# A hybrid decoder layer on one core: output weights split once into device memory, opening output groups started early, SP loads reordered

## The chip, the core and the metric

The kernel runs on one core of a Trainium2 chip. The core has five engines with instruction streams of their own: TensorE (PE, matmuls from SBUF into PSUM), VectorE (DVE), ScalarE (ACT), GpSimd (POOL) and SyncE (SP, which here only issues DMAs). ACT and POOL issue DMAs too. The metric is device time in microseconds of one execution, lower is better. Before the change it is 1189.5 us, the median of three runs.

## The reference

One decoder layer for 1024 prompt tokens and 8 x 8 sample tokens (1088 in all), model width 1024, float32. One input projection feeds two mixers, retention (8 heads of 64, in chunks of 128 tokens) and sliding-window attention (8 query heads, 2 key heads, window 128, with sinks). Their outputs, side by side, go through one output projection with a residual, and then comes an MLP of width 4096 with squared ReLU:

```
o_r = rms_norm(retention(q_r, k_r, v_r)) * silu(g_r)
o_s = sliding_window_attention(q_s, k_s, v_s, sinks)
h = x + concatenate([o_r, o_s], axis=-1) @ w_out
hf = rms_norm(h, norm_ffn_gain)
y = h + square(relu(hf @ w_up)) @ w_down
```

The retention state and the last window of keys and values are outputs too.

## The kernel before

Everything is kept with features on partitions and tokens along the free side. A float32 product is made of three matmul passes on operands of type float32r: each operand is split into a high part (an ACT cast) and a low part (DVE or POOL subtracts the high part), and `mm3` (lines 174 to 177) multiplies high by high, low by high and high by low.

The stages follow each other in the program, but a planner in the tile library orders each engine's instructions at build time by a simulated clock and the program's order as priority. Tiles with one tag share a fixed number of places (`bufs`). A tile in a reused place waits until the readers of the earlier tile are done. Pools on one side of SBUF are stacked, and a pool opened after another was closed takes the same space. `tc.issue_after(x)` puts the instructions traced in its block behind `x` on `x`'s engine.

The order of the program:

1. Projections for the attention part, then eight window-attention blocks, `swa_block` (line 378). Each uses two score tiles `s` (ring of 3 places of 4 KB per partition) and two transposed tiles `pt` (ring of 2). Then the sample tokens' attention with one more `s` tile, `s8` (line 464).
2. Projections of retention queries, keys and gates, which are stored in device memory (lines 509 to 528). They also serve PE as work while the attention chain waits for the other engines. Then `attn.close()`.
3. Retention. Its pools `ret` and `retv` take the space of the attention pools. `ret_load` (line 540) brings a block's queries, keys and gates on the SP queue. Nine value blocks (`value_block`, line 590) and the sample tokens' steps (`retention_decode`) are put in a written order on PE with `queued`. `retention_block(t)` (line 698) does eight blocks in sequence, because each uses the state of the one before it: cast and subtraction of queries and keys (lines 705 to 710), scores, decay, values, state, then a norm (`head_norm`, line 611). `mix_block` (line 766) transposes the result, multiplies by the gate and splits it into the mix operands `mix[s, "rh"]` and `mix[s, "rl"]`.
4. The output projection, in two halves of tokens, `s` = 0 and 1, each in 8 groups `m` of 128 output features. A group has two PSUM tiles (`h` = 0, 1) and, for each, 12 matmuls with the attention mix (`"a"`) and 12 with the retention mix (`"r"`). The first half needs the mix of blocks 0 to 4 only, and its groups are put between blocks 5, 6 and 7 with `out_early`; the second half follows when retention is done. The attention mix comes back from device memory with `mix_load`.
5. The MLP, `up` for 16 pairs and then the down projection, which make up most of the span.

The weights of the output projection reach it so: `wo_pair` (line 819) loads 512 KB of two groups' raw rows on SP into a `raw` tile and splits each with `wsplit` (ACT cast, DVE subtraction, ring `wa` of 4). As both token halves need all weights, each raw weight is loaded and split twice, 32 splits of 128 x 512 in all. `wo_pair`'s pool `mw` is opened after `proj.close()`, in the space of the projection weights. The first raw loads of the up projection (line 1073 on, `r0` and `s56`) use the same `raw` ring of `mw`.

Of the kernel before, what the change touches and what calls it, by code (L numbers as in the profile page):

```python
# [11 lines left out]
F32 = mybir.dt.float32  # L12
F32R = mybir.dt.float32r
# [7 lines left out]
P = 128  # L21
# [15 lines left out]
def hymba_layer(ctx: ExitStack, tc: tile.TileContext, a: dict, o: dict):  # L37
# [90 lines left out]
    g_d = scratch.tile([P, 4, T], F32, name="g_d")  # L128
    ms_hi_d = scratch.tile([P, 4, T], F32, name="ms_hi_d")
    ms_lo_d = scratch.tile([P, 4, T], F32, name="ms_lo_d")  # L130
    y_d = scratch.tile([P, 4, 4, 2, Q], F32, name="y_d")
    u_d = [scratch.tile([P, 2, 2, 7, Q], F32, name=f"u_d{g}") for g in range(8)]

# [302 lines left out]
            )  # L436


    pr = psB.tile([P, 512], F32, tag="t2", name="prq8")
    for t4 in range(4):  # L440
        col_sums(pr[:, t4 : t4 + 1], q8s[:, t4, :], ones[:, 0:1])
# [19 lines left out]
        nc.sync.dma_start(d_, a[s_])  # L461
    nc.sync.dma_start(o["kc"][:, :, 0:120], kc[:, :, 8:128])
    nc.sync.dma_start(o["vc"][0:120], vc[8:128])
    s8 = sp.tile([P, 4, 256], F32, tag="s", name="s8", bufs=3)[:, :, :192]
    for tt in range(2):
        ps = psB.tile([P, 512], F32, tag="t1", name="sc8")
        for t4 in (2 * tt, 2 * tt + 1):
# [230 lines left out]
    def retention_block(t):  # L698
        nonlocal state
        nm = f"r{t}"  # L700
        vt = vts[t]
        qt, kt, gt = ret_load(t, ((rv, 2), (mxr, 1) if t in (3, 6) else (rv, 2)))

        pts = []
        nc.scalar.copy(kh, kt)
        nc.gpsimd.tensor_tensor(kl, kt, kh.bitcast(F32), ALU.subtract)
        for hh in range(2):
            q_ = slice(hh * 64, hh * 64 + 64)
            nc.scalar.copy(qbh[q_, :, hh, :], qt[q_])
            nc.vector.tensor_tensor(qbl[q_, :, hh, :], qt[q_], qbh[q_, :, hh, :].bitcast(F32), ALU.subtract)  # L710
        for i in range(2):
            ps = psB.tile([P, 512], F32, tag="t1", name="rs" + nm)
            for p_ in (2 * i, 2 * i + 1):
                cc = (p_ % 2) * 256
                mm3(ps[:, cc : cc + 256], kh[:, p_, :], kl[:, p_, :], qbh[:, p_, :, :], qbl[:, p_, :, :], True, True)
            pt = rp.tile([P, 4, 128], F32, tag="rpt", name="rpt" + nm, bufs=3)
            nc.vector.tensor_tensor(
                pt, ps.rearrange("p (h l) -> p h l", h=4), intra[:, 4 * i : 4 * i + 4, :], ALU.mult
            )
            pts += [pt[:, h, :] for h in range(4)]  # L720
        kd, _ = scaled_keys(kt, kdec, nm)

        po = psB.tile([P, 512], F32, tag="t3", bufs=1, name="ro" + nm)
        for h in range(8):
            for q_ in (slice(0, 64), slice(64, 128)):
                nc.tensor.matmul(
                    po[q_, h * 64 : h * 64 + 64], pts[h][:, q_], vt[:, h * 64 : h * 64 + 64],
                    start=h == 0, stop=h == 7 and t == 0,
                )
        if t:  # L730
            qd = rv.tile([P, 4, 128], F32, tag="qd", name="qd" + nm, bufs=1)
            nc.gpsimd.tensor_tensor(qd, qt, qdec, ALU.mult)
            for p_ in range(4):
                nc.tensor.matmul(
                    po[:, p_ * 128 : p_ * 128 + 128], qd[:, p_, :],
                    state[:, p_, :, :].rearrange("p h e -> p (h e)"), start=False, stop=p_ == 3,
                )
        pu = psB.tile([P, 512], F32, tag="t2", name="pu" + nm)
        for h in range(8):
            q_ = slice((h % 2) * 64, (h % 2) * 64 + 64)  # L740
            nc.tensor.matmul(
                pu[q_, (h // 2) * 64 : (h // 2) * 64 + 64], kd[:, h * 64 : h * 64 + 64], vt[:, h * 64 : h * 64 + 64],
                start=True, stop=True,
            )
        puv = pu[:, :256].rearrange("p (q e) -> p q e", q=4)
        new = states[t % 2]
        for hh in range(2):
            q_ = slice(hh * 64, hh * 64 + 64)
            if t == 0:
                nc.vector.tensor_copy(new[q_, :, hh, :], puv[q_])  # L750
            else:
                for p_ in range(4):
                    nc.vector.scalar_tensor_tensor(
                        new[q_, p_, hh, :], state[q_, p_, hh, :], sdec[q_, p_ : p_ + 1], puv[q_, p_, :],
                        ALU.mult, ALU.add,
                    )
        state = new
        if t == NB - 1:
            for hh in range(2):
                nc.sync.dma_start(o["st"][hh * 64 : hh * 64 + 64], state[hh * 64 : hh * 64 + 64, :, hh, :])  # L760

        mt = rv.tile([P, 512], F32, tag="mt", name="mt" + nm)
        head_norm(po, mt, slice(0, 128), nm)
        return mt, gt
# [42 lines left out]
        return raw  # L807


    mix, acc, fs, last_out = {}, {}, {}, [None]  # L810

    def mix_load(s, pl):
        for x, d_ in zip("hl", (ms_hi_d, ms_lo_d)):
# [4 lines left out]

    def wo_pair(s, m, half):

        raw = mw.tile([P, 1024], F32, tag="raw", name=f"wo{half}{s}_{m}_raw", bufs=3)
        c0 = 512 * (half == "a")
        nc.sync.dma_start(
            raw.rearrange("p (m n) -> p m n", m=2), a["w_out"][m : m + 2, :, c0 : c0 + 512].rearrange("m p n -> p m n")
        )
        for i in range(2):
            yield wsplit(raw[:, i * 512 : i * 512 + 512], "wa", f"wo{half}{s}_{m + i}", nc.vector)

    def out_half(s, half, ps, h, w, first, last):
        for k in range(4):  # L830
# [4 lines left out]
    def residual(s, m, pss):  # L835
        y = om.tile([P, 2, Q], F32, tag="y", name=f"y{s}_{m}", bufs=2)
        nc.gpsimd.dma_start(y.rearrange("p h n -> p (h n)"), a["xY"][:, s, m, :])
        for h in range(2):
            nc.vector.tensor_tensor(y[:, h, :], pss[h], y[:, h, :], ALU.add)
        kk, k2 = m % 4, m // 4  # L840
        nc.gpsimd.dma_start(y_d[:, 2 * k2 : 2 * k2 + 2, kk, s, :], y)
        if m > 5 and s == 0:
            f = mx0.tile([P, 2, Q], F32, tag=f"f{m}", name=f"f{s}_{m}")
        else:
            f = om.tile([P, 2, Q], F32, tag=f"f{min(m, 4)}", name=f"f{s}_{m}", bufs=1 + m // 4)
        fs[s, m] = f
        nc.scalar.activation(f, y, AF.Copy, scale=g_ffn[:, m : m + 1])

        def squares():
            if m == 0:  # L850
                acc[s] = mw.tile([P, 2, Q], F32, tag="acc", name=f"acc{s}")
                nc.scalar.activation(acc[s], y, AF.Square)
            else:
                sq = om.tile([P, 2, Q], F32, tag="sq", name=f"sq{s}_{m}")
                nc.scalar.activation(sq, y, AF.Square)
                nc.vector.tensor_tensor(acc[s], acc[s], sq, ALU.add)

        return squares
# [55 lines left out]
            nc.scalar.copy(rsf[:, s, h, :], pb[:, :Q])  # L914


    def queued(ins, f, *args):
        with tc.issue_after(ins):
            return f(*args)
# [24 lines left out]
    qbh, qbl, kh, kl = split_space([ring.tile([P, 1024], F32R, tag="raw", name=f"qk{i}", bufs=3) for i in range(3)])  # L944
    for i, x in enumerate("hl"):
        mix[0, "r" + x] = slot(6 + i, F32R, "mixr" + x)[:, : 8 * Q].rearrange("p (k h n) -> p k h n", k=4, h=2)
    held, mxr, mxrx = {}, None, ExitStack()
    for t in range(5):
        if t == 0:
            for _ in range(2):  # L950
# [8 lines left out]
        if t == 3:  # L959
            sl8c = slot(8, F32R, "qkb")  # L960
            qbh, qbl, kh, kl = split_space([sl8c[:, i : i + 1024] for i in (0, 1024, 2048)])
        if t:
            mix_block(t - 1, *held[t - 1])
        held[t] = retention_block(t)
        if 0 < t < 4:
            ins = queued(ins, value_block, t + 4)
    proj.close()
    mw = ctx.enter_context(pool("mw", side="right"))
    rsf = mw.tile([P, 2, 2, Q], F32, tag="rsf", name="rsf")
    ox = ExitStack()  # L970
    om = ox.enter_context(pool("o", side="right"))
    for x in "hl":
# [1 line left out]
    mxA = ox.enter_context(pool("mxA", side="right"))  # L974
    mx0x = ExitStack()
    mx0 = mx0x.enter_context(pool("mx0", side="right"))
    early = lambda: psA.tile([P, 512], F32, tag="mm", name="pso")[:, :Q]

    def out_early(m):

        if m and m % 2 == 0:
            gens["a"], gens["r"] = (wo_pair(0, m, x) for x in "ar")
            ahead.extend(next(gens[x]) for x in "ar")
        wa_, wr_ = ahead
        ahead.clear()
        if m % 2 == 0:
            ahead.extend(next(gens[x]) for x in "ar")
        pss = [early() for h in range(2)]
        for h in range(2):
            out_half(0, "a", pss[h], h, wa_, True, False)  # L990
            out_half(0, "r", pss[h], h, wr_, False, True)
        residual(0, m, pss)()

    gens = {x: wo_pair(0, 0, x) for x in "ar"}
    ahead = [next(gens[x]) for x in "ar"]
    mix_block(4, *held[4])
    for t in (5, 6, 7):
        mt = retention_block(t)
        for m in (2 * t - 10, 2 * t - 9):
            out_early(m)  # L1000
        if t == 6:
            with tc.issue_after(last_load[0].ins):
                mix_load(1, mxA)
        mix_block(t, *mt)
# [394 lines left out]
```

## Time and profile before

| what | value |
|---|---|
| median of three runs | 1189.5 us (1188.86 to 1191.59) |
| profiled execution: its time | 1188.43 us |
| profiled execution: its span, first to last instruction | 1186.7 us |
| granted TensorE clock | 1.00 |
| attention blocks end | about 263 us |
| retention and first output half | about 290 to 450 us |
| MLP begins | about 496 us |

The profile shows one execution. Busy times of the engines overlap, and a busy PE is not PE at its peak, since the end of a matmul is modelled and matmuls overlap in its pipeline. So stretches are read by the number of matmuls in them and by the waits of PE, not by PE's share alone. In a row of instructions, "x" counts them, `out<-in` names the tiles, and the bracket gives the idle time before and what ended it.

### The profile page before, as it was taken

What the parts mean: (1) busy time and instruction counts of PE and PEld (TensorE: products, weight loads), DVE (VectorE), ACT (ScalarE), POOL (GpSimd) and SP (SyncE); (2) the same over time, 40 slices, a digit from 0 to 9 for tenths busy, and PEclk for the clock granted to TensorE, in tenths of its full rate; (3) what the DMA queues carried; (4) which work ended last, traced back from release to release, by engine and by line L of the source; (5) the groups of instructions that cost most, each with busy time, mean ns of one, the idle gap of its engine ahead of it and who ended that gap; (6) DMA issues with size and microseconds to landing.
All of it is one profiled execution on the core that took longest, in us unless ns stands there. A gap on an engine that the chain in (4) does not pass through costs nothing.

```text
span 1186.7 us, 23488 instructions
## 1 busy us (share of the span) xinstructions
PE 1169.6 (99%) x9405; PEld 1123.5 (95%) x9405; DVE 839.1 (71%) x1546; ACT 513.8 (43%) x1055; POOL 494.2 (42%) x393
## 2 busy tenths in 40 slices
PE   8999999999999999999999999999999999999998
PEld 7999988989778899999999999999989999999998
DVE  7556868632257769887766667666788787888676
ACT  8343544553334347644444444444642333333231
POOL 0125333332255542467666666566383142053000
PEclk9999999999999999999999999999999999999999
DMA  7221235333525555343444434444685456443225
GB/s 247 73 62 68 93 102 166 104 115 98 180 74 168 181 183 156 113 156 133 141 151 148 144 130 141 151 148 157 236 290 157 148 169 203 143 155 104 76 59 187
DMA packets 102277, 169.44 MB, mean 143 GB/s; under 512 B 12000, under 2 KB 68256, under 8 KB 101912
## 3 DMA queue, kind: packets, MB, share of 16 engines
q1 hardware_dynamic: 88807, 123.80, 31.5%
q10 hardware_dynamic: 10800, 35.23, 9.3%
q0 software_dynamic: 2560, 8.91, 2.3%
q8 instruction: 74, 1.21, 0.4%
q14 instruction: 36, 0.29, 0.1%
HBM read 114.30 MB, written 53.61 MB: 142 GB/s over the span
## 4 chain that ended last, share of the span: by engine, by line
PE 81%; DVE 6%; DMA 5%; issue 3%; ACT 2%; POOL 2%; SPq 0%; ACTq 0%; DVEq 0%; POOLq 0%
PE psd L176 9%; PE psd L177 9%; PE psd L175 9%; PE psx L175 5%; PE psx L177 5%; PE psx L176 5%; PE psz L175 2%; PE psz L177 2%; PE psz L176 2%; PE pst L175 2%; PE pst L176 2%; PE pst L177 2%; PE psf L175 2%; PE psf L177 2%; PE psf L176 2%
## 5 line engine op out<-in xcount | busy, mean ns | idle before, releaser
L175 PE MATMUL psd<-uh,wd_w 128*128 128x272 f32 x896 | 258.4, 288 | 3.2 <-DVE a L1267 2.4
L176 PE MATMUL psd<-uh,wd_w 128*128 128x272 f32 x896 | 259.3, 289 | 0.0
L177 PE MATMUL psd<-ul,wd_w 128*128 128x272 f32 x896 | 257.9, 288 | 0.7 <-DVE ul L792 0.7
L175 PEld LDWEIGHTS psd<-uh,wd_w 128*128 128x128 f32 x896 | 169.1, 189 | 4.3 <-DVE a L1267 3.4
L177 PEld LDWEIGHTS psd<-ul,wd_w 128*128 128x128 f32 x896 | 168.7, 188 | 0.9 <-DVE ul L792 0.9
L176 PEld LDWEIGHTS psd<-uh,wd_w 128*128 128x128 f32 x896 | 168.4, 188 | 0.0
L1267 DVE TENSOR_TENSOR a<-a,psd 128x272 f32<-128x272 f32 x248 | 101.9, 432 | 48.9 <-PE psd L177 48.8
L792 DVE TENSOR_TENSOR wu_w<-wu_s,wu_w 128x512 fp32r<-128x512 f32 x64 | 61.9, 971 | 49.8 <-ACT wu_w L791 49.2
L791 ACT CAST wd_w<-wd_s 128x512 fp32r<-128x512 f32 x64 | 37.5, 621 | 119.0 <-PE psd L177 107.2
L792 DVE TENSOR_TENSOR ul<-ur,uh 128x1088 fp32r<-128x1088 f32 x56 | 84.0, 1527 | 4.1 <-ACT uh L791 4.1
L1120 DVE SCALAR_TENSOR_TENSOR m<-m,rsf 128x272 f32<-128x272 f32 x96 | 72.9, 760 | 3.2 <-ACT rsf L914 0.5
L175 PE MATMUL psx<-op_1h,wu_w 128*128 128x272 f32 x256 | 74.3, 290 | 0.4 <-ACT m L1136 0.4
L177 PE MATMUL psx<-op_1l,wu_w 128*128 128x272 f32 x256 | 74.1, 289 | 0.0
L175 PE MATMUL psx<-op_0h,wu_w 128*128 128x272 f32 x256 | 74.1, 290 | 0.0
L177 PE MATMUL psx<-op_0l,wu_w 128*128 128x272 f32 x256 | 74.1, 289 | 0.0
L176 PE MATMUL psx<-op_1h,wu_w 128*128 128x272 f32 x256 | 73.7, 288 | 0.0
L176 PE MATMUL psx<-op_0h,wu_w 128*128 128x272 f32 x256 | 73.7, 288 | 0.0
L365 POOL TENSOR_TENSOR sp<-sp,ssp 128x1024 f32<-128x1024 f32 (+1 forms) x16 | 28.6, 1787 | 88.4 <-DVE ssp L364 60.1
L791 ACT CAST uh<-ur 128x1088 fp32r<-128x1088 f32 x56 | 59.7, 1101 | 12.7 <-PE psd L176 9.1
L175 PE MATMUL psf<-hnh,wqk_hi 128*128 128x384 f32 (+1 forms) x192 | 63.5, 331 | 0.2 <-DVE qkst L517 0.2
L177 PE MATMUL psf<-hnl,wqk_hi 128*128 128x384 f32 (+1 forms) x192 | 63.2, 329 | 0.0
L176 PE MATMUL psf<-hnh,wqk_lo 128*128 128x384 f32 (+1 forms) x192 | 62.8, 327 | 0.0
(343 smaller groups left out, 3619.4 us busy)
## 6 DMA issues: line engine op xcount, KB each, us to landing
ur<-u_d SPq DMA_DIRECT2D x53, 544.0 KB, 5.2
u_d<-r4t SPq DMA_DIRECT2D x32, 544.0 KB, 4.6
wu_r<-in_w_up ACTq DMA_DIRECT2D x32, 512.0 KB, 4.4
wd_r<-in_w_down ACTq DMA_DIRECT2D x30, 512.0 KB, 6.5
u_d<-r3t SPq DMA_DIRECT2D x32, 408.0 KB, 2.9
y<-in_xY POOLq DMA_DIRECT2D x16, 272.0 KB, 3.5
y_d<-y POOLq DMA_DIRECT2D x16, 272.0 KB, 3.2
yt<-y_d SPq DMA_DIRECT2D x16, 272.0 KB, 2.9
```

What stands on the lines that cost most here:

```text
L175: nc.tensor.matmul(ps, lh, rh, start=first, stop=False, skip_group_check=more)
L176: nc.tensor.matmul(ps, ll, rh, start=False, stop=False, skip_group_check=more)
L177: return nc.tensor.matmul(ps, lh, rl, start=False, stop=last, skip_group_check=more)
L365: nc.gpsimd.tensor_tensor(s, s, ss.unsqueeze(2).broadcast_to([P, 4, n]), ALU.mult)
L791: nc.scalar.copy(hi, src)
L792: lo_eng.tensor_tensor(lo, src, hi.bitcast(F32), ALU.subtract)
L1120: nc.vector.scalar_tensor_tensor(t_, src, 0.0, rsf[:, s, h, :], ALU.max, ALU.mult)
L1267: added[i] = nc.vector.tensor_tensor(to, to, ps, ALU.add).ins
```

## The change

Four edits go together.

- Behind the attention blocks in the program, each of the eight raw weight rows `w_out[m]` (512 KB) is loaded into an `s` tile and split in two column halves into `pt` tiles with high and low part side by side; POOL's queue stores them in a new tensor `wo_d` in device memory, 16 stores of 512 KB. The tile `s8` of the sample attention is taken before them in the program.
- `wo_pair` loads split weights from `wo_d`, 512 KB for one group and half, in place of a raw load and two splits. Its tiles take four places `wa` and the three places `raw` in turn, seven in all. The loads are listed in `w_loads`.
- The attention half of the groups 0 and 1 of the first token half is taken out of `out_early`: the weights are loaded in block 3 into the projection ring's `raw` tiles, and the matmuls (four PSUM tiles, three of `psA` and one of `psB`'s tag `t1`) come behind block 4 in the program, ahead of `proj.close()`. `out_early(0)` and `out_early(1)` then add the retention half alone.
- On SP, the loads of queries, keys and gates of blocks 6 and 7 are put behind the latest load in `w_loads`, and the attention mix of the second token half is loaded in block 7 in place of block 6. The tile `acc0` is taken when `mw` is opened.

```diff
+    wo_d = [scratch.tile([P, 2, 1024], F32, name=f"wo_d{m}") for m in range(8)]
...
+    s8 = sp.tile([P, 4, 256], F32, tag="s", name="s8", bufs=3)[:, :, :192]
+    for m in range(8):
+        raw = sp.tile([P, 4, 256], F32, tag="s", name=f"wo_raw{m}", bufs=3).rearrange("p k n -> p (k n)")
+        nc.sync.dma_start(raw, a["w_out"][m])
+        for c in (slice(0, 512), slice(512, 1024)):
+            w = sp.tile([P, 2, 512], F32R, tag="pt", name=f"wo_hl{m}")
+            nc.scalar.copy(w[:, 0, :], raw[:, c])
+            nc.vector.tensor_tensor(w[:, 1, :], raw[:, c], w[:, 0, :].bitcast(F32), ALU.subtract)
+            nc.gpsimd.dma_start(wo_d[m][:, :, c], w.bitcast(F32))
...
-        qt, kt, gt = ret_load(t, ((rv, 2), (mxr, 1) if t in (3, 6) else (rv, 2)))
+        with tc.issue_after(w_loads[-1].ins) if t > 5 else ExitStack():
+            qt, kt, gt = ret_load(t, ((rv, 2), (mxr, 1) if t in (3, 6) else (rv, 2)))
...
     def wo_pair(s, m, half):
 
-        raw = mw.tile([P, 1024], F32, tag="raw", name=f"wo{half}{s}_{m}_raw", bufs=3)
         c0 = 512 * (half == "a")
-        nc.sync.dma_start(
-            raw.rearrange("p (m n) -> p m n", m=2), a["w_out"][m : m + 2, :, c0 : c0 + 512].rearrange("m p n -> p m n")
-        )
         for i in range(2):
-            yield wsplit(raw[:, i * 512 : i * 512 + 512], "wa", f"wo{half}{s}_{m + i}", nc.vector)
+            tag, bufs = ("raw", 3) if len(w_loads) % 7 > 3 else ("wa", 4)
+            w = mw.tile([P, 2, 512], F32R, tag=tag, name=f"wo{half}{s}_{m + i}", bufs=bufs)
+            w_loads.append(nc.sync.dma_start(w.bitcast(F32), wo_d[m + i][:, :, c0 : c0 + 512]))
+            yield w
...
+    def early(n):
+        pl, tag, bufs = (psA, "mm", 3) if n < 3 else (psB, "t1", 2)
+        return pl.tile([P, 512], F32, tag=tag, name="pso", bufs=bufs)[:, :Q]
...
         if t == 3:
...
+            for m in range(2):
+                opening.append(ring.tile([P, 1024], F32R, tag="raw", name=f"woa0_{m}", bufs=3))
+                nc.sync.dma_start(
+                    opening[m].bitcast(F32).rearrange("p (i n) -> p i n", i=2), wo_d[m][:, :, 512:1024])
...
+    for m in range(2):
+        w = opening[m].rearrange("p (i n) -> p i n", i=2)
+        opened.append([early(2 * m + h) for h in range(2)])
+        for h in range(2):
+            out_half(0, "a", opened[m][h], h, w, True, False)
     proj.close()
     mw = ctx.enter_context(pool("mw", side="right"))
...
+    acc = {0: mw.tile([P, 2, Q], F32, tag="acc", name="acc0")}
...
     def out_early(m):
 
-        if m and m % 2 == 0:
-            gens["a"], gens["r"] = (wo_pair(0, m, x) for x in "ar")
-            ahead.extend(next(gens[x]) for x in "ar")
-        wa_, wr_ = ahead
-        ahead.clear()
         if m % 2 == 0:
-            ahead.extend(next(gens[x]) for x in "ar")
-        pss = [early() for h in range(2)]
+            gens = {x: wo_pair(0, m, x) for x in "ar"[not m :]}
+            ahead.extend({x: next(gens[x]) for x in gens} for i in range(2))
+        w = ahead.pop(0)
+        pss = opened[m] if m < 2 else [early(h) for h in range(2)]
         for h in range(2):
-            out_half(0, "a", pss[h], h, wa_, True, False)
-            out_half(0, "r", pss[h], h, wr_, False, True)
+            if m > 1:
+                out_half(0, "a", pss[h], h, w["a"], True, False)
+            out_half(0, "r", pss[h], h, w["r"], False, True)
         residual(0, m, pss)()
...
-        if t == 6:
+        if t == 7:
             with tc.issue_after(last_load[0].ins):
                 mix_load(1, mxA)
```

More of the change, by code (lines that the diff above doesn't have):

```diff
@@ L463, in hymba_layer @@
     nc.sync.dma_start(o["vc"][0:120], vc[8:128])
-    s8 = sp.tile([P, 4, 256], F32, tag="s", name="s8", bufs=3)[:, :, :192]
     for tt in range(2):
@@ L807, in rawload @@
         return raw
-    mix, acc, fs, last_out = {}, {}, {}, [None]
+    mix, fs, last_out = {}, {}, [None]
     def mix_load(s, pl):
@@ L850, in squares @@
             if m == 0:
-                acc[s] = mw.tile([P, 2, Q], F32, tag="acc", name=f"acc{s}")
+                if s:
+                    acc[s] = mw.tile([P, 2, Q], F32, tag="acc", name=f"acc{s}")
                 nc.scalar.activation(acc[s], y, AF.Square)
@@ L946, in hymba_layer @@
         mix[0, "r" + x] = slot(6 + i, F32R, "mixr" + x)[:, : 8 * Q].rearrange("p (k h n) -> p k h n", k=4, h=2)
-    held, mxr, mxrx = {}, None, ExitStack()
+    opening, opened = [], []
+    held, mxr, mxrx, w_loads = {}, None, ExitStack(), []
     for t in range(5):
@@ L976, in hymba_layer @@
     mx0 = mx0x.enter_context(pool("mx0", side="right"))
-    early = lambda: psA.tile([P, 512], F32, tag="mm", name="pso")[:, :Q]
     def out_early(m):
-        if m and m % 2 == 0:
-            gens["a"], gens["r"] = (wo_pair(0, m, x) for x in "ar")
-            ahead.extend(next(gens[x]) for x in "ar")
-        wa_, wr_ = ahead
-        ahead.clear()
         if m % 2 == 0:
-            ahead.extend(next(gens[x]) for x in "ar")
-        pss = [early() for h in range(2)]
+            gens = {x: wo_pair(0, m, x) for x in "ar"[not m :]}
+            ahead.extend({x: next(gens[x]) for x in gens} for i in range(2))
+        w = ahead.pop(0)
+        pss = opened[m] if m < 2 else [early(h) for h in range(2)]
         for h in range(2):
-            out_half(0, "a", pss[h], h, wa_, True, False)
-            out_half(0, "r", pss[h], h, wr_, False, True)
+            if m > 1:
+                out_half(0, "a", pss[h], h, w["a"], True, False)
+            out_half(0, "r", pss[h], h, w["r"], False, True)
         residual(0, m, pss)()
-    gens = {x: wo_pair(0, 0, x) for x in "ar"}
-    ahead = [next(gens[x]) for x in "ar"]
+    ahead = []
     mix_block(4, *held[4])
```

## The prediction

> **What bounds the kernel now.** The page's first part comes first: one engine is busy for nearly the whole span.
>
> ```profile
> span 1186.7 us, 23488 instructions
> PE 1169.6 (99%) x9405; PEld 1123.5 (95%) x9405; DVE 839.1 (71%) x1546; ACT 513.8 (43%) x1055; POOL 494.2 (42%) x393
> ```
>
> TensorE (PE) idles 1186.7 - 1169.6 = 17.1 us. The diff leaves its matmuls as they are, so it can only fill holes in PE or make new ones. The table by stretches says where holes are; columns are time, length, PE, weight loads, VectorE (DVE), ScalarE (ACT), POOL, granted clock, DMA share, GB/s.
>
> ```profile
> 380.00:400.00 20.00, 18.64 (x215) 17.34 (x214) 14.95 (x37) 5.63 (x10) 10.30 (x8) 1.00 0.66 216
> 400.00:420.00 20.00, 18.66 (x182) 17.91 (x181) 15.97 (x33) 10.00 (x17) 9.88 (x11) 1.00 0.42 127
> 500.00:520.00 20.00, 19.06 (x195) 18.68 (x195) 16.08 (x31) 11.96 (x29) 9.23 (x7) 1.00 0.27 94
> 560.00:580.00 20.00, 20.00 (x161) 20.00 (x160) 14.03 (x21) 9.19 (x21) 14.39 (x14) 1.00 0.44 152
> ```
>
> The steady stretch 560 to 580 has no hole, at clock 1.00. In it a matmul starts every 20 / 161 = 0.124 us. The retention stage loses 1.36 + 1.34 us, the start of the MLP 0.94. PE's waits name the causes: instruction <- releaser, total, times, longest.
>
> ```profile
> PE pm L771 <- DVE mtr L619: 1.3, 1, 1.3
> PE rsr L175 <- ACT qkb L709: 1.2, 1, 1.2
> PE psz L176 <- DVE wu_w L792: 0.9, 1, 0.9
> PE pur L741 <- DVE kdr L605: 0.2, 1, 0.2
> ```
>
> The first two holes have a DMA behind them, as the chain of waits shows (start, length, what):
>
> ```profile
> 376.00 5.34 DMA qt<-qr_d
> ...
> 382.07 0.69 DVE qkb L710
> 382.76 0.09 DVE orrr L617
> ...
> 391.37 9.25 DMA qt<-qr_d
> ```
>
> The query tile of block six lands late, and DVE's norm for an earlier block queues behind the split of that tile; then the tile of block seven takes 9.25 us, because SP issued it right behind two large loads:
>
> ```profile
> 389.96 0.63 SPq L815 DMA_DIRECT2D mixah<-ms_hi_d  x1
> 390.64 0.63 SPq L815 DMA_DIRECT2D mixal<-ms_lo_d  x1
> 391.37 0.57 SPq L546 DMA_DIRECT2D qt<-qr_d  x1
> ```
>
> **The change part by part.** *What it can win.* Three retention holes: 1.3 + 1.2 + 0.2 = 2.7 us. A drained PE pays again, since a matmul that the trace shows with 0.288 us starts every 0.124 us when fed; each refill costs about 0.16 us.
>
> ```profile
> L175 PE MATMUL pso<-mixah,woa x128: 282/288/397, 373.1 to 489.6; 128*128 128x272 f32 x128
> ```
>
> So 2.7 + 3 x 0.16 = 3.2 us. Three edits work on them. Four opening groups (4 x 12 matmuls, 48 x 0.124 = 6.0 us) have their weights in ring tiles from block three on, so PE has work while a tile is late. The mix load moves behind block seven's loads, which removes the 9.25 us landing. The splits leave the stage: 32 ACT casts and 32 DVE subtractions.
>
> ```profile
> L792 DVE TENSOR_TENSOR wor<-wor_raw,wor x16: 680/690/1768, 374.8 to 487.6; 128x512 fp32r<-128x512 f32 x16
> ```
>
> ```profile
> L791 ACT CAST woa<-woa_raw x16: 603/620/624, 371.6 to 478.1; 128x512 fp32r<-128x512 f32 x16
> ```
>
> At the medians that is 32 x 0.69 = 22.1 us of DVE and 32 x 0.62 = 19.8 us of ACT between 366 and 490. Neither bounds PE there, so it counts for nothing except shorter queues ahead of the norm and the query splits. If that cover were gone it would be worth its whole length, which no row supports.
>
> *What it adds.* The split runs once: 16 casts (9.9 us ACT), 16 subtractions (11.0 us DVE), 8 loads of 512 KB on SP and 16 stores of 512 KB on POOL's queue. A POOL issue takes 0.73 us, so 11.6 us of POOL.
>
> ```profile
> L841 POOL DMA_DIRECT2D y_d<-y x16: 717/726/795, 402.7 to 500.4; - x16
> ```
>
> ```profile
> 260.00:280.00 20.00, 20.00 (x198) 17.70 (x197) 7.37 (x23) 7.00 (x15) 4.91 (x4) 1.00 0.39 115
> 280.00:300.00 20.00, 20.00 (x145) 16.99 (x145) 3.52 (x7) 4.48 (x7) 8.80 (x8) 1.00 0.48 139
> 300.00:320.00 20.00, 20.00 (x117) 16.96 (x116) 3.89 (x5) 5.71 (x8) 3.47 (x3) 1.00 0.57 164
> ```
>
> When does it run? Its tiles come in program order after the eight window-attention blocks, in rings of three (`s`) and two (`pt`). The trace suggests that ring places are given in program order: the sums for the sample heads (prq, L155) had their last input at 229.0 but ran only from 261.6, after all eight blocks.
>
> ```profile
> L433 DVE COPY q2v<-rsb x8: 171/175/176, 228.3 to 229.0; 1x64 f32<-1x64 f32 x8
> ```
>
> ```profile
> L155 PE MATMUL prq<-ones,q2v x64: 165/178/191, 261.6 to 264.0; 128*32 128x1 f32 x32, 1*32 1x1 f32 x32
> ```
>
> ```profile
> 261.74 1.08 PE L421 MATMUL po<-ptp,q2v 128*64 128x512 f32 x4
> ```
>
> So the splits start near 262.8, when the last block's `pt` tiles are read. There ACT, DVE and POOL are mostly idle. One turn of a `pt` place is cast 0.62 + subtraction 0.69 + landing. Landings of that size: 4.6 us for 544 KB on SP, 3.2 us for 272 KB on POOL; a 512 KB store between them by size takes 4.4 us.
>
> ```profile
> u_d<-r4t SPq DMA_DIRECT2D x32, 544.0 KB, 4.6
> ...
> y_d<-y POOLq DMA_DIRECT2D x16, 272.0 KB, 3.2
> ```
>
> A turn is 5.7 us; 16 tiles through two places are 8 turns, 45.6 us, so the last store lands at about 308.4. The Trainium skill ("DMA: Bandwidth & Descriptors", Anatomy of one DMA) fits a POOL-queue DMA as 2.0 us plus bytes over 436 GB/s; that estimate is 3.2 us for 512 KB, a turn of 4.5 and an end near 299. The trace is slower than that fit: 3.2 where it gives 2.6.
>
> Who needs the space? The retention pools lie over the attention pools. By the tile sizes, the value tiles lie over `s`, and the decayed sample keys and the first retention queries over `pt`. PE's order there is written out, and the fourth value block starts at 315.60 and needs a PSUM bank that the first one's evacuation frees; the sample state update needs the keys at 322.29.
>
> ```profile
> L597 ACT ACTIVATE vtr<-pst,rst x8: 668/687/689, 302.7 to 368.0; 128x512 f32<-128x512 f32 x8
> ```
>
> ```profile
> 411.29 0.61 DVE kdr L605
> ```
>
> ```profile
> 315.60 0.48 PE L175 MATMUL pst<-wv_hi,hnh 128*128 128x512 f32 x1
> ...
> 322.29 1.08 PE L688 MATMUL pur<-s0v,kdr 64*64 64x512 f32 x4
> ```
>
> The last raw tile is free one landing before the end, 304.0, and its value tile (0.69) is written by 304.7, 10.9 us early; the keys (0.61) are ready by 309.0, 13.3 us early. So I cost the new part at zero; bounds are 0 and the second rival.
>
> *Reloads.* 30 loads of 512 KB (14 for the first half, 16 for the second) and two for the opening replace 16, so 8.4 MB more between 365 and 500: 62 GB/s on top of the rows' 94 to 216 GB/s. Landings of that size:
>
> ```profile
> woa_raw<-in_w_out SPq DMA_DIRECT2D x8, 512.0 KB, 4.8
> wor_raw<-in_w_out SPq DMA_DIRECT2D x8, 512.0 KB, 4.1
> ```
>
> ```profile
> L823 SPq DMA_DIRECT2D wor_raw<-in_w_out x8: 367/371/460, 366.9 to 468.1; - x8
> ```
>
> A weight tile feeds 24 matmuls, 3.0 us, and seven places are there ahead of use: hidden, cost 0. Without that cover each would show as up to 4.8 - 3.0 = 1.8 us.
>
> *Queues.* The loads of blocks six and seven are put behind the weight loads on SP; DVE, ACT and PE of the block wait for them. At 0.37 us an issue this is hidden by the opening groups. These hold four PSUM banks, one of which block five's scores lack: its two halves go one after the other, while PE has the groups' other halves to do. At the MLP's start the last weights share the `raw` ring with the first up-weights, whose sums now wait for matmuls instead of splits; two subtractions less on DVE, 1.4 us, pull the other way. I leave the 0.9 us hole there as it is; bounds -1.1 (0.9 + 0.16, gone) and +2.6: the second raw load may start only when the matmuls of its place end, at about 489.9 - 24 x 0.124 = 486.9, lands 4.1 later at 491.0, and the sums started at 488.39 before.
>
> ```profile
> 488.39 5.71 POOL L1075 TENSOR_TENSOR wu_s<-wu_r 128x512 f32<-128x512 f32 x1 [0.73 <-DVE wor L792]
> ```
>
> *Sum.* The third hole, 0.2 + 0.16, hangs on the keys, which the change only helps by shorter queues; I take half of it: -3.2 + 0.2 = -3.0. The profiled execution took 1188.43 us with a span of 1186.7, and the median of three is 1189.5. From the median: **1186.5 us**.
>
> **The rivals.** *The holes only move (no change).* Block seven's tile no longer stands behind two mix loads of 1088 KB, 2176 KB together, but behind four weight loads of 512 KB, 2048 KB together, which is as much. For it: where the loads are issued in one burst, the landing stays near 9 us. Against it: the seven places are free early and the loads can land before. The opening groups also give PE no more before the mix than the four banks hold. Time: 1189.5, or 1188 with half of it won.
>
> *The stores are late (slower).* The place is PE's written order from 315.6 to 322.3. The split moves 4.2 MB in and 8.4 MB out; over 45.6 us that is 276 GB/s on top of 115 to 164, about 415. The most that this trace shows in a stretch is 358, with share 1.04, and a 544 KB load took 10.59 us there:
>
> ```profile
> 860.00:880.00 20.00, 18.68 (x146) 18.25 (x146) 16.78 (x21) 11.52 (x20) 19.19 (x11) 1.00 1.04 358
> ```
>
> ```profile
> 856.66 10.59 DMA ur<-u_d
> ```
>
> So landings will stretch. From 6.0 us (a turn of 7.3, end at 321.2) the cover is gone, and each further 1 us of landing costs 8 turns less one, 7 us. At 7.0 us the end is 329.3, the last raw tile is free at 322.3, the value tile at 323.0: PE stands 7.4 us, and the time is 1186.5 + 7.4 = 1193.9. The same comes earlier if the third raw tile must wait for the place of the sample scores, read at 281.93:
>
> ```profile
> 281.93 1.04 PE L370 MATMUL pps<-c_ident,s 128*128 128x128 f32 x8
> ```
>
> Then six turns of 5.7 follow a load of 4.1 from 283.0: end 321.3, value tile 317.6, 2.0 us lost already; with landings of 6 us 9.7 us. The Trainium skill (same page, SWDGE vs HWDGE vs iDMA) says that DVE can lock POOL out while POOL writes its descriptors; here the POOL issues took 0.717 to 0.795 us in a busy DVE stage, so no row shows such a delay, and I give it no price.
>
> *The MLP's start gets worse.* The up-weight sums come 2.6 us later and nothing takes it up: 1186.5 + 2.6 = 1189.1.
>
> **How the numbers follow.** My forecast has 0.38, the moved holes 0.26, the late stores 0.28, the MLP's start 0.08. A measurement of this kernel tells apart about 0.2%, 2.4 us. Under 1187.1 is faster: most of the forecast and a little of the rest, 0.39. Over 1191.9 is slower: most of the late stores, 0.24, and 0.05 for the other rivals' far ends, 0.29. Between: 0.32. The range goes from 1184.0 (all three retention holes and the MLP's hole won, with a little besides) to 1195.0 (late stores at a little over 7 us); about 0.2 lie outside, most of it above.
>
> **What would show it.** Right: PE at 19.9 or more in 380 to 420, no wait of pm on mtr or of rsr on qkb, the last wo_d store landed before 316, and no PE idle from 285 to 330. Wrong: a wait of the value matmuls on vtr or of pur on kdr near 316 to 325 (late stores); a qt landing of 8 us or more behind weight loads (moved holes); PE under 19 in 500 to 520 with wu_s later than 495. The placing falls if the splits are seen much earlier than 262, between the attention blocks.

## The result and the profile after

The changed kernel takes 1218.26 us (median of 4 runs, 1215.28 to 1219.15), beside 1189.18 us for the kernel before in the same session. The ratio is 1.0238, with a 95% interval from 1.0219 to 1.0257: it is slower by 29 us, where the prediction said 3 us faster and ended its range at 1195.0.

The profiled execution took 1219.15 us with a span of 1217.4 us, 30.7 more than the span before. First the waits of PE in the changed kernel (instruction <- releaser: total, times, longest), to be read beside those quoted in the prediction:

```profile
PE sc L485 <- DVE s L490: 10.4, 1, 10.4
PE pps L371 <- POOL s L366: 9.9, 1, 9.9
PE rsr L643 <- DMA kt<-kr_d: 6.7, 1, 6.7
...
PE pso L176 <- DVE y L849: 1.5, 1, 1.5
...
PE psz L177 <- DVE wu_w L803: 0.9, 1, 0.9
PE po L504 <- DVE pt L499: 0.8, 1, 0.8
```

The waits that the change was to remove (pm for mtr, rsr for qkb, pur for kdr) are gone; one of 1.5 us (the output sums for y) is new in their stage. Far larger are four new ones: 10.4 + 9.9 + 0.8 + 6.7 = 27.8 us. None is at a load of output weights, and the last is at retention's first keys. The first stands at the **sample attention**, the short softmax over the sample heads between the last window block and retention. The table by stretches (columns as in the prediction) shows where:

```profile
280.00:300.00 20.00, 14.29 (x72) 12.04 (x70) 6.48 (x8) 7.09 (x11) 8.95 (x8) 0.91 0.61 215
300.00:320.00 20.00, 4.60 (x46) 2.97 (x48) 8.00 (x17) 6.58 (x15) 5.31 (x6) 0.50 0.49 188
...
420.00:440.00 20.00, 18.49 (x204) 17.59 (x203) 14.51 (x31) 6.48 (x12) 9.48 (x10) 1.00 0.92 310
```

In 300 to 320 PE is busy for 4.60 of 20 us (before: 20.00), and the granted clock is 0.50. The DMA share there is only 0.49, so the transfers do not fill the engines. Four groups of the trace (form: shortest/median/longest ns, first to last start) say what ran when: the sample scores' scaling into the tile s in the changed kernel and in the kernel before, then the split.

```profile
L490 DVE SCALAR_TENSOR_TENSOR s<-smp,nsl,sc x4: 406/414/415, 304.3 to 306.3; 128x192 f32<-128x192 f32 x4
```

```profile
L480 DVE SCALAR_TENSOR_TENSOR s<-smp,nsl,sc x4: 408/414/415, 267.0 to 271.8; 128x192 f32<-128x192 f32 x4
```

```profile
L443 SPq DMA_DIRECT2D wo_raw<-in_w_out x8: 333/333/1386, 236.7 to 297.3; - x8
```

```profile
L446 ACT CAST wo_hl<-wo_raw x16: 602/617/622, 262.3 to 313.4; 128x512 fp32r<-128x512 f32 x16
L447 DVE TENSOR_TENSOR wo_hl<-wo_raw,wo_hl x16: 678/693/2240, 263.0 to 314.1; 128x512 fp32r<-128x512 f32 x16
L448 POOL DMA_DIRECT2D wo_d<-wo_hl x16: 678/690/822, 264.0 to 316.0; - x16
```

The raw loads begin at 236.7, when the first place of `s` comes free, and the eighth goes out at 297.3. The tile of the sample scores, which shares the ring `s` with them, is first written at 304.3 instead of 267.0. The timeline of VectorE at that point (start, length, what; in brackets the idle time before and its releaser):

```profile
303.53 0.69 DVE L447 TENSOR_TENSOR wo_hl<-wo_raw,wo_hl 128x512 fp32r<-128x512 f32 x1 [5.09 <-ACT wo_hl L446]
304.26 0.74 DVE L490 SCALAR_TENSOR_TENSOR s<-smp,nsl,sc 128x192 f32<-128x192 f32 x2
```

The score goes in 0.04 us after this subtraction, the twelfth of the 16, has read the sixth raw tile for the last time and so given its place back. From there the chain of waits leads to retention:

```profile
305.90 3.29 DMA wo_d<-wo_hl
...
309.26 0.15 ACT wo_hl L446
...
309.89 1.28 ACT L359
...
314.15 1.93 POOL s L366
...
316.12 1.98 PE pps L371 x8
...
322.28 0.52 SPq L376
...
323.60 0.59 SPq L556
...
324.23 4.17 DMA kt<-kr_d
...
328.53 1.57 PE rsr L643 x16
```

The reader sees each in-order queue pass the lateness on. ACT's exponentials (L359) stand behind a cast that waited for a store to land; POOL's normalization (L366) comes after them; PE then transposes, the result is stored (L376), and only behind that store does SP issue the first retention tiles. The first rsr starts 30.0 us later than before (328.5 against 298.5).

Most of the 9.9 us wait for POOL is not lateness that the queues add, but the length of the softmax itself. Its first step on DVE (the row maximum) and its last on POOL (the normalization), before and then in the changed kernel:

```profile
L350 DVE TENSOR_REDUCE mxs<-s x1: 953/953/953, 272.2 to 272.2; 128x4 f32<-128x768 f32 x1
L365 POOL TENSOR_TENSOR s<-s,sss x1: 1467/1467/1467, 278.4 to 278.4; 128x768 f32<-128x768 f32 x1
```

```profile
L351 DVE TENSOR_REDUCE mxs<-s x1: 953/953/953, 306.8 to 306.8; 128x4 f32<-128x768 f32 x1
L366 POOL TENSOR_TENSOR s<-s,sss x1: 1921/1921/1921, 314.1 to 314.1; 128x768 f32<-128x768 f32 x1
```

From the start of the first to the end of the second it takes 7.6 us before and 9.3 us here. Before, PE had other matmuls to do meanwhile; here the last of those had ended at 294.3.

### The profile page after: what moved, and what is told of

The parts are those of the page before. It is cut to its first block, busy times and chain, and to the rows that moved or that the text cites. A ratio compares the mean times of both kernels' runs of the same rounds, so it can differ in the third digit from the quotient of the medians.

```text
span 1217.4 us, 23557 instructions
## 1 busy us (share of the span) xinstructions
PE 1173.8 (96%) x9405; PEld 1126.4 (93%) x9405; DVE 827.1 (68%) x1530; ACT 504.0 (41%) x1038; POOL 497.5 (41%) x409
## 4 chain that ended last, share of the span: by engine, by line
PE 81%; DVE 7%; issue 4%; DMA 3%; POOL 2%; ACT 2%; SPq 0%; ACTq 0%; POOLq 0%; DVEq 0%
PE psd L178 8%; PE psd L177 8%; PE psd L176 8%; PE psx L176 5%; PE psx L178 4%; PE psx L177 4%; PE pso L176 3%; PE pso L178 3%; PE pso L177 2%; PE psz L176 2%; PE psz L178 2%; PE psz L177 2%; PE pst L176 2%; PE psf L176 2%; PE psf L178 2%
## 5 line engine op out<-in xcount | busy, mean ns | idle before, releaser
L366 POOL TENSOR_TENSOR sp<-sp,ssp 128x1024 f32<-128x1024 f32 (+1 forms) x16 | 28.6, 1789 | 88.4 <-DVE ssp L365 60.0
```

The source lines that it names most:

```text
L366: nc.gpsimd.tensor_tensor(s, s, ss.unsqueeze(2).broadcast_to([P, 4, n]), ALU.mult)
```

## The experiments

**Whose place, and when.** The theory after reading the traces, T1: the raw tiles hold the places that the sample scores need, and the lateness does the rest. T2: the split's own traffic and queue work cost what they cost, wherever it stands. Three runs come first.

e1 gives the scores a place of their own:

```
-    s8 = sp.tile([P, 4, 256], F32, tag="s", name="s8", bufs=3)[:, :, :192]
+    s8 = sp.tile([P, 4, 192], F32, tag="s8", name="s8", bufs=1)
     for m in range(8):
```

> The sample scores' tile s8 gets a place of its own, so that the eight raw weight tiles have the three places of `s` to themselves; all else is as in the changed kernel. T1 (the raw tiles, which need nothing, take the places that s8 needs, and the sample attention is written only when the last raw tile has its place; all the lost time hangs on that): the 10.4 us wait of PE for s (sample scores) is gone, s8's first write runs near 268 us and not at 304, the later waits of 9.9 us (PE for the normalized probabilities) and 6.7 us (for kt) shrink to under 2 us together, the clock stays at 1.00, and the time is 1184 to 1192 us. T2 (the split costs what it costs by its own traffic: 4.2 MB in and 8.4 MB out between 237 and 319 us keep queues, POOL and the retention places late wherever the sample scores stand): the 10.4 us wait goes, but PE stands as long at the next tile that needs a place or a load, and the time stays above 1205 us.

Measured: 1204.4 us, ratio 1.0123 (1.0106 to 1.0140). Half of the loss went, and half stayed, so neither expected time held. The scores were written from 268.8, as T1 said, and the two waits at the sample attention fell from 20.3 to 0.8 us:

```profile
PE rsr L643 <- DMA kt<-kr_d: 5.5, 1, 5.5
...
PE ror L664 <- DVE rptr L648: 3.0, 1, 3.0
```

The rest now sits in retention. SP's queue shows one way:

```profile
296.52 0.52 SPq L376 DMA_DIRECT2D ms_lo_d<-mls  x1
301.20 0.33 SPq L443 DMA_DIRECT2D wo_raw<-in_w_out  x1
301.63 0.59 SPq L556 DMA_DIRECT2D qt<-qr_d  x1
```

The stores of the sample's result had been issued by 297.04, but the retention tile goes out at 301.63, behind the last raw load, which waits for a place. The splits run on to 318.8 (last cast; 313.4 in the changed kernel).

e2 moves the whole block in the program behind the sample attention; the scores share `s` as in the change:

```
     mix_store(mh, ml, 1024, 64)
+    for m in range(8):
+        raw = sp.tile([P, 4, 256], F32, tag="s", ...)
...
```

> The block that loads, splits and stores the weights is moved in the program to behind the sample attention; s8 still takes its place in `s`, which the raw tiles share. T1 (a place goes to whichever tile's first write is ready first, whatever the program says): the raw loads need nothing and are issued as early as in the changed kernel (near 237 us), s8 is written again only after 300 us, time above 1208 us. T3 (places go by program order, as my prediction had it, and the changed kernel only put the splits ahead of the sample attention): the first raw load waits until s8 has its place, s8 is written near 268 us, the last store lands later than 319 us, and the time is below 1200 us unless retention then waits for the places.

Measured in one execution: 1211.28 us. T1 as worded fell, though its time was right: the first raw load went out at 266.6, not near 237, and the sample attention was on time (scores from 266.9). That is T3, with its reservation that retention may wait. Taken together, these two kernels say that the order of places follows the order of first writes in the program. In the changed kernel the scores' tile is created above the loop, but its first write stands below it; there it came last, and here first. The time stayed high because the last raw load was still later, and the retention loads behind it (first stretch: two raw loads):

```profile
299.84 7.47 SPq L511 DMA_DIRECT2D wo_raw<-in_w_out  x2
307.43 0.59 SPq L557 DMA_DIRECT2D qt<-qr_d  x1
```

PE waited 16.3 us for kt there.

e3 issues the stores on SP instead of POOL (`nc.sync.dma_start(wo_d[m]...` for `nc.gpsimd.dma_start`).

> The 16 stores of the split weights are issued on SP's queue instead of POOL's; s8 still shares `s`. T1: the 10.4 us wait for the sample scores stays (9 to 13 us), since the raw tiles still take the places; of the 9.9 us wait for POOL's normalization a part goes (POOL no longer has the stores ahead of it: 16 x 0.69 = 11 us of issues between 264 and 316 us), but SP's raw loads now queue behind stores that wait for splits, so the time is 1210 to 1222 us. T2 (POOL's in-order queue is the cause): both waits fall by more than half and the time is below 1200 us.

Measured in one execution: 1208.89 us, just under T1's 1210; its 9 to 13 us for the first wait were wrong, and T2's time (below 1200) too. The splits ended 7 us sooner (last cast at 306.1), and the scores got their place sooner (first written at 297.1):

```profile
PE pps L371 <- POOL s L366: 9.1, 1, 9.1
PE rsr L643 <- DMA kt<-kr_d: 6.2, 1, 6.2
...
PE sc L485 <- DVE s L490: 3.0, 1, 3.0
```

The 9.1 us wait for POOL's normalization stayed with no store left on POOL. So POOL's issues were not its cause. From the row maximum (299.6) to the end of the normalization (308.2) the softmax took 8.6 us here, and PE again had nothing else to do.

**How much is split.** e6 splits only groups 0 to 3 (`for m in range(4)`, and `wo_d[(m + i) % 4]` at the loads), with the scores in their own place. It leaves out half of the weights, so its output is not the layer's, and it serves only to read the time.

> Only the first four weight groups are loaded, split and stored, and groups 4 to 7 of the output use the same four (so the output is of other weights, with as many loads and matmuls); the sample scores have a place of their own. T1 (what is left of the loss with the scores' own place, 15 us, hangs on when the split ends, and not on how much it moves): the last raw load is issued near 267 us instead of 301, the retention loads go out on SP near 291 to 295 us as before, kt is waited for by less than 1 us, and the time is 1185 to 1190 us. T2 (the loss goes with the traffic): half of it stays, 1194 to 1199 us.

Measured: 1184.44 us, ratio 0.9961 (0.9944 to 0.9977). Half of the traffic takes away all of the loss, not half of it. The last store went out at 290.7 and kt was waited for 0.4 us:

```profile
L448 POOL DMA_DIRECT2D wo_d<-wo_hl x8: 674/693/822, 263.7 to 290.7; - x8
```

e7 makes a complete kernel of it: groups 0 to 3 are split once and stored, groups 4 to 7 are split at their use as before.

```
-    for m in range(8):
+    for m in range(4):
...
     def wo_pair(s, m, half):
...
+        if m >= 4:
+            raw = mw.tile([P, 1024], F32, tag="raw", ...)
+            w_loads.append(nc.sync.dma_start(...))
         for i in range(2):
+            if m >= 4:
+                yield wsplit(raw[:, i * 512 : i * 512 + 512], "wa", ..., nc.vector)
+                continue
```

> A complete version: the sample scores have their own place, the weight groups 0 to 3 are split once and stored as in the changed kernel, and groups 4 to 7 are loaded raw and split where they are used, in both halves, as in the kernel before. T1: it keeps what the four-raws run had up to 440 us (no wait for s, POOL or kt; the retention holes gone), and pays for the 16 subtractions of 0.69 us on DVE from block seven on only if y stands behind them: 1185 to 1188 us. T3 (the gain of the four-raws run came from the work that it left out): 1188 to 1192 us.

Measured: 1183.24 us, ratio 0.9951 (0.9938 to 0.9965): **0.5% faster than the kernel before**, and 35 us faster than the changed one. It is 1.8 us under the 1185 of T1, and far from T3's 1188 to 1192.

e8 is the same with six groups.

> As the version with four groups kept, but with six groups split ahead of retention and two split at use. T1 (the loss starts where the split's end passes the point at which retention's first loads go out on SP, near 293 us, and its places are needed, near 310 us, and then grows by about one turn of the places for each further group, 6 to 7 us): six groups end near 305 us, so the last raw load is near 286 us and SP is not held up; kt is waited for by under 2 us, and the time is 1186 to 1192 us. T2 (the loss grows evenly with the traffic, 15 + 5 us over four groups): 1194 to 1196 us.

Measured: 1190.16 us, ratio 1.0003 (0.9991 to 1.0015), as T1 said. With eight groups and the scores in their own place it was 1204.4 (e1). So from four to six groups the cost is 3.5 us a group, from six to eight 7.1. In e8 SP is clear (kt goes out at 296.38 and is waited for by 1.0 us), yet retention's second query tile comes late. Its issue on SP in e8, then in e7:

```profile
312.22 0.52 SPq L556 DMA_DIRECT2D qt<-qr_d  x1
```

```profile
298.84 0.52 SPq L556 DMA_DIRECT2D qt<-qr_d  x1
```

That tile lies over the attention space. In e8 it goes out 13.4 us later than in e7, 0.1 us after the last store, issued at 309.0, has landed at 312.1 (in e7 that store was issued at 292.1). In e1 it is the same: the last store lands at 323.5, and the second query tile goes out at 323.6.

**Where else the splits could stand.** e4 puts one group's split behind each of the eight window blocks; e10 does the same and gives the scores their own place.

```
     for c in range(NB):
         done_swa.append(swa_block(c))
+        wo_split(c)
```

> The split of one weight group (one raw load, two casts, two subtractions, two stores) stands in the program behind each of the eight window-attention blocks, not all eight behind the last; tiles and queues are as in the changed kernel, and the sample scores take their place last. T1 (all the loss is lateness: whatever stands behind the last raw tile, its places and SP's order, is late, and the traffic itself costs nothing): the splits run between about 130 and 270 us, where PE had no hole before, the sample scores get their place before 275 us, the waits for s (10.4), POOL's normalization (9.9) and kt (6.7) go, the clock stays at 1.00 and the time is 1185 to 1191 us. T2 (the split costs by its traffic and its work on ACT, DVE and POOL): the blocks' own tiles now wait for places and engines, holes of 15 us or more in all appear between 130 and 270 us, and the time is above 1200 us.

> The splits of all eight groups stand between the window-attention blocks, as in the run that did so, and the sample scores have a place of their own. T1 (there too it was the scores' place that cost most): the 4.9 us wait for s goes and POOL's 7.7 us with it, the retention loads go out on SP before 300 us, and the time is 1187 to 1197 us. Rival (the blocks themselves are late by the stores that hold their `pt` places, block seven's last read being near 288 us instead of 262): the sample sums and the retention start later whatever s8 has, and the time stays at 1200 to 1210 us.

Measured: e4 1212.74 us, ratio 1.0199 (1.0182 to 1.0216); e10, in one execution, 1211.47 us. T1's time failed in both. T2 was right on e4's time, but not on the holes: PE idled for 2.4 us between 120 and 280, not 15. The rival given with e10 fits, though the time is 1.5 us above its range: the waits for s (4.9 us) and for POOL (7.6 us) are as in e4, since the blocks came late. The last transposed tile of the window blocks, on DVE before and in e10:

```profile
L412 DVE COPY ptp<-ppp x16: 659/688/693, 121.4 to 256.5; 128x512 f32<-128x512 f32 x16
```

```profile
L413 DVE COPY ptp<-ppp x16: 661/692/693, 121.5 to 288.6; 128x512 f32<-128x512 f32 x16
```

It is 32.1 us late: each block needs both places of `pt`, and there the stores hold them while they land. In e10 the copies into ptp wait 21.9 us in all for stores of wo_d; before, they wait for no store. The sample attention is then late whatever place it has.

**The rest of the change without the split.** e5 leaves the split where it was before (at each use) and keeps the opening groups, with their weights split in the ring, and the queue edits.

> Everything of the change but the split: the weights are split again where they are used, as before; the four opening groups (their weights loaded and split in the ring from block three on), the loads of blocks six and seven behind the weight loads, and the later mix load stay. T1: none of the 28 us of waits between 293 and 328 us is there, the clock is 1.00 there, and the time is 1185 to 1190 us; if my terms for the retention stage hold, 1186 to 1187.5. T3 (the opening groups and the queues carry part of the 29 us): above 1195 us.

Measured: 1195.21 us, ratio 1.0058 (1.0040 to 1.0075), just beyond T3's bound of 1195, and none of the waits of 293 to 328 us is there. T3 held, not T1. PE loses 6.8 us in two waits of output sums for y, whose addition stands on DVE behind splits (PE's waits, then DVE's timeline):

```profile
PE pso L175 <- DVE y L843: 6.8, 2, 3.7
```

```profile
386.54 3.48 DVE L711 TENSOR_TENSOR qkb<-qt,qkb 64x512 fp32r<-64x512 f32 x2
390.04 1.64 DVE L793 TENSOR_TENSOR woa<-woa_raw,woa 128x512 fp32r<-128x512 f32 x1
...
392.21 0.42 DVE L843 TENSOR_TENSOR y<-pso,y 128x272 f32<-128x272 f32 x1
```

The opening groups hold four PSUM banks until y is added; with the splits still on DVE that is worse than no opening groups. With the split ahead of time the same wait is 1.5 us, and 1.4 without the opening groups (e12).

**Which edit brings the gain.** From e7, e9 undoes the later mix load (`if t == 6:`), and e12 the opening groups.

> The version with four groups kept, with one edit of the change undone: the second mix load goes out in block six again. T1 (the mix load behind block seven's loads is what took the wait of rsr for qkb away): the query tile of block seven lands 2 to 4 us later behind it and a hole of about 1 us comes back near 390 us: 1 to 2 us slower than with four groups kept. T3 (the opening groups alone cover that hole): the same time within 0.5 us.

> The version with four groups kept, without the four opening groups: the weights of groups 0 and 1 are loaded at their use in out_early as the others are, and PE gets no output matmuls ahead of the mix. T1 (the opening groups are what PE does while a tile or a norm is late): the waits of pm for mtr and of rsr for qkb, or waits like them, come back with 1 to 2.5 us in 370 to 410 us, and the time is 1184.5 to 1187 us. T3 (the lighter DVE and ACT queues alone closed the holes): 1182.5 to 1184 us, no such wait.

Measured: e9 1184.82 us, ratio 0.9961 (0.9949 to 0.9973); e12 1184.97 us, ratio 0.9963 (0.9950 to 0.9977). Both intervals overlap e7's, so the times do not order the three, though both medians lie where T1 put them. In e9 no wait of rsr for qkb came back, and PE in 380 to 400 was 18.48 as in e7: against that wait the later mix load was not needed. In e12 small waits came back, less than T1's 1 to 2.5 us, the one below and one of 0.4 us for a load of woa:

```profile
PE rsr L178 <- DVE qkb L721: 0.5, 1, 0.5
```

Where e7's gain stands is not shown. In its profiled execution the first pm (the transposition that begins the mix) starts 2.7 us later than before, the first psx (the MLP's first sums) 0.6 us later, and the end comes 3.4 us sooner. So 2.1 us are won between pm and psx, but 4.0 us from psx on, in the MLP. Of these, 0.9 us is the wait at the MLP's start, which is gone; the rest stands in code that the change leaves alone, and no run takes it apart. e9 and e12 win 2.9 and 2.6 us there.

**Was it SP's order?** e11 is e1 with the raw loads on POOL's queue.

> All eight groups split at once with the sample scores in their own place, and the eight raw loads issued on POOL's queue instead of SP's, so that the first retention loads no longer stand on SP behind the last raw load. T1 (SP's order held kt up by 5.5 us): qt and kt go out right behind the sample's mix stores, near 296 to 298 us, kt is waited for by under 2 us; the waits that hang on the split's end (3.0 us for DVE's rptr, the later query tiles for the places of `pt`) stay, and POOL's own work may be later by a few us: 1195 to 1202 us. Rival (kt's space, not SP's order, was late): kt goes out after 300 us all the same, 1203 us or more.

Measured in one execution: 1198.68 us, the time as expected, the reason not. Here the sample's result was stored 3.1 us later than in e1 (first store issued at 298.3 against 295.2), kt went out right behind it at 300.4, as the rival said, and was waited for 7.2 us. So this run does not tell SP's order from the lateness of the sample attention, and how e1's 15 us divide between SP's order, the places and the clock **stays open**. That the loss goes with the split's end, and not in proportion to what is moved, is what e6, e7 and e8 show: nothing of it is left at four groups, and from there it grows.

## Why the prediction was wrong

**The failed step** is "So I cost the new part at zero". The new part cost 29.1 us. The step counted the cover to the value tiles at 315.6 and the keys at 322.3 and looked at the sample scores only as an early owner of a place that the third raw tile waits for. The program order of places was right as a rule, and gave the splits' start (262.8 predicted, first cast 262.3). It was applied to the wrong line: what counts is the first write, which for the scores stands behind the loop. So the raw tiles did not wait for the scores; the scores came behind all eight raw tiles in the order of places, and were written at 304.3 instead of 267.0. e1 puts this at 1218.3 - 1204.4 = 13.9 us. The other 15.2 us go with the split's end. The rival "the stores are late" was priced at 7.4 us, or 9.7 with its sub-case (10.0 by its own figures: 283.0 + 4.1 + 6 x 7.3 - 6.0 + 0.7 - 315.6).

**The second error is the turn.** It was 5.7 us, so the last store was to land at 308.4. The 16 subtractions ran from 263.0 to 314.1, about 7.5 turns of two places: 6.8 us a turn. The page of the changed kernel has the landing:

```profile
wo_d<-wo_hl POOLq DMA_DIRECT2D x16, 512.0 KB, 5.0
```

5.0 us instead of 4.4 explains 0.6 of the 1.1; the rest was not taken apart. The Trainium skill's fit ("DMA: Bandwidth & Descriptors", Anatomy of one DMA), quoted in the prediction for 3.2 us, was further off than the rows for this median. The trace agrees with it only at the end: the five stores issued from 304.5 on, when SP's loads were in, landed in 3.1 to 3.3 us, the eleven before them in 4.5 to 6.6. The rival "stores are late" had the right kind of cause, but its threshold came too late. Retention's second query tile is needed in `pt` space near 298.8 (e7), long before 315.6, so the cover in that step was not there; e8, with a last store issued at 309.0, already pays 7 us against e7.

**A term that was missing is the clock.** In 5 us stretches of the changed kernel:

```profile
290.00:295.00 5.00, 4.29 (x19) 3.21 (x18) 0.90 (x2) 0.00 (x0) 1.41 (x2) 1.00 0.70 243
295.00:300.00 5.00, 0.00 (x0) 0.00 (x0) 1.38 (x2) 1.82 (x3) 1.38 (x2) 0.65 0.48 165
...
325.00:330.00 5.00, 1.47 (x16) 1.41 (x16) 0.35 (x1) 0.00 (x0) 2.10 (x5) 0.50 0.91 258
```

PE's last matmul ends at 294.3; at 296.5 the granted clock falls to 0.50, and it stays there to 334.0. From the first rsr to the first pm the kernel before needs 347.0 - 298.5 = 48.5 us, the changed one 381.1 - 328.5 = 52.6: 4.1 us more without a wait. Of that stretch 5.5 us (to 334.0) and another 3.4 (from 340.9, see the last section) run at half clock; half of them is 4.5 us, an estimate that covers the 4.1. The Trainium skill ("TensorE: Matmul & The Clock Gate", Part 1) gives half rate after an idle window of about 3.4 us. The trace agrees with the half rate, but the fall came sooner, 2.2 us after the last matmul. In the clock records of these traces the stretches at half clock last 37.55 us here, 10.24 in e8 and 3.41 in e7, whole multiples of 3.41.

**What was right.** The retention stage was won in part. From the first pm to the first psx (rows: first to last start; before, then e6):

```profile
L771 PE MATMUL pm<-c_ident,mtr x32: 271/273/328, 347.0 to 432.9; 128*128 128x128 f32 x32
...
L175 PE MATMUL psx<-op_0h,wu_w x256: 283/289/373, 496.0 to 835.5; 128*128 128x272 f32 x128
```

```profile
L782 PE MATMUL pm<-c_ident,mtr x32: 270/272/328, 346.7 to 429.5; 128*128 128x128 f32 x32
...
L176 PE MATMUL psx<-op_0h,wu_w x256: 285/289/372, 492.5 to 830.8; 128*128 128x272 f32 x128
```

That is 149.0 us before and 145.8 in e6, 3.2 us less. The forecast had 3.0. In the changed kernel itself the stretch is 147.0 (381.1 to 528.1) and in e7 146.9 (349.7 to 496.6), 2.0 and 2.1 us less: the three holes of 2.7 us are gone, but the wait for y, which the prediction did not have, takes 1.5 us back. Without the opening groups (e12) it is 148.1, without the split 156.6 (e5), with the mix load in its old place 146.9 (e9). So in this stretch, by one profile each, the stored split and the opening groups work together, and the mix load's place showed nothing. The reloads cost nothing that shows: 512 KB loads of stored weights landed in 5.9 and 5.4 us, and no wait on them stands in the changed kernel. "The holes only move" was half right: 2.7 us of waits became 1.5 in the changed kernel and e7, and 0.4 in e6. Its sign showed, a query tile that took 8.4 us behind weight loads, but PE did not wait for it. The MLP's start kept its 0.9 us wait in the changed kernel and lost it in e7.

Of the four signs of being right, one held (no wait of pm on mtr or of rsr on qkb) and three failed: the last store landed at 319.1, PE idled between 285 and 330, and PE in 420 to 440, within the counterpart of 380 to 420, was 18.49 and not 19.9. Of the signs for the late stores, a wait for vtr or kdr, neither appeared: PE stood at the sample attention, which no sign named.

The sums meet. At the first rsr the changed kernel is 30.0 us behind (27.8 in the four waits; the sample attention's matmuls, at half clock, take about 3 us more than before, which covers the other 2.2), at the first pm 34.1, at the first psx 528.1 - 496.0 = 32.1, and at the end 30.7. The last 1.4 us come from the MLP, whose code the change leaves alone; why it is shorter is not known.

## What to carry to other kernels

Before work is put into a ring that others use, list the ring's users by their **first write** in program order, not by where the tile is made: a short task with a late first write gets its place after a long loop above it. Then follow each in-order queue (here ACT, DVE and SP) to the next stage, and price the lateness at the first thing that needs the space or the queue, not at the tiles one had in mind. And when a wait looks like a queue's fault, first measure how long the work behind it takes when nothing is late: here it was mostly the softmax's own length, which other matmuls had hidden. An idea that costs in full may pay in part: with half of the weights split ahead, the split ended before anybody needed the room.

## What was not expected of the hardware

The clock also fell without a long stop of PE. In e7 PE was busy, by the profile's modelled ends, in every stretch of 1 us from 308 to 315; two of them:

```profile
308.00:309.00 1.00, 1.00 (x12) 1.00 (x11) 0.00 (x0) 0.32 (x1) 1.00 (x1) 1.00 0.66 167
...
311.00:312.00 1.00, 1.00 (x4) 0.81 (x3) 0.00 (x0) 0.00 (x0) 0.00 (x0) 0.50 0.00 0
```

3.4 us at half clock (309.9 to 313.3) follow the small 64x64 matmuls of ror, which began at 306.5 there; the changed kernel shows the same dip at 340.9, 3 us after its ror at 337.9. The kernel before runs the same matmuls at 305.4 with a granted clock of 1.00 throughout, and so do e6, e9 and e12, whose code in that stretch is that of e7. So these matmuls alone do not bring the dip, and why it comes in some executions stays open.
